# Sixteen tokens move from the dense expert sum to row fetches, and one-hots are built four tokens at a time

## The chip, the cores and the metric

The kernel runs on one core of a Trainium2 chip. The core has a matmul engine (TensorE, PE in the rows; its weight loads are PEld), a vector engine (VectorE, DVE), an activation engine (ScalarE, ACT), GpSimd (POOL) and SyncE (SP); 16 DMA engines move data for all of them. The metric is the device time of one execution in microseconds (us), as the median of several runs.

## The reference, cut to what matters

Two transformer blocks run one after the other on 512 tokens of 1024 numbers. The change lies in the feed-forward part of the first block: 16,384 experts, each one row of `u_tab` and one row of `v_tab`. For each token and each of 8 heads the 16 best experts are found through product keys (an expert's number is `128*i1 + i2`); `g` are their softmaxed scores, the gates. All is float32.

```python
        eidx = jnp.take_along_axis(cidx, fpos, axis=-1).reshape(C, PEER_HEADS * PEER_TOPK)
        g = jax.nn.softmax(fv, axis=-1).reshape(C, PEER_HEADS * PEER_TOPK)
        u = u_tab[eidx]
        a = jax.nn.gelu(jnp.einsum('ted,td->te', u, hb).astype(jnp.float32), approximate=False)
        coef = (g * a).astype(hb.dtype)
        vv = v_tab[eidx]
        return jnp.einsum('te,ted->td', coef, vv)
```

So each token uses 128 expert rows of each table. A convolution block and an attention block follow, which need the whole result.

## The kernel before, in words

`phase_peer` computes these experts in two ways. The first `ND` = 384 tokens are **dense**: every expert is computed for all of them, and a gate matrix that is mostly zeros picks what counts. The last 128 tokens are **fetched**: one token sits on each partition, and for each of its 128 experts an indirect DMA issued by GpSimd brings one row per token (128 rows of 4 KB, 512 KB in all) into a buffer.

The dense tokens pass through two stages of 128 units each. In the **first stage** a unit is 128 experts of `u`: a slab of 512 KB is loaded (`_load`), split into a high and a low half (`_split`: `whi` on ScalarE, `wlo` on VectorE), multiplied with the tokens (`gemm_w`: 8 blocks of rows, three matmuls each by `mm3`, with `ND` columns moving), and its Gelu goes to `ga`, which is written to DRAM (`Ad`). In the **second stage** a unit is 128 experts of `v`: `weight(i)` multiplies gates (`gg`, read back from DRAM, or the last two chunks `near`, which stay in SBUF) with `ga` and splits the product (`w_hi`, `w_lo`); then 8 blocks of `mm3` add into the 8 PSUM banks `y`, again with `ND` columns moving. The last two units run as one, bank by bank. Then each bank gets the fetched tokens' sum by a transpose of `yG` into its last columns (L1280), and VectorE adds the bank to the residual `xres2` (L1281), from which the convolution starts (`act`, L384 and L385).

The gate matrix is made during the first stage, in steps of four tokens in `gates(tb)`: per token one-hots of `i1` (times the gate) and of `i2`, and a matmul of the two (`flush`, L1099), in chunks of 32 tokens (`gc`, to DRAM as `Gd`).

The fetches are one generator, `gather()`: for each head 16 fetches of `u` rows into `ug`, each multiplied with the token `hG` and summed by one VectorE instruction (L1143), a Gelu over the 16 sums, then 16 fetches of `v` rows into `vg`, each added into `yG` by one VectorE instruction (L1153). `ug` and `vg` are rings of 3 buffers each; a fetch waits on GpSimd until the VectorE instruction that used its buffer is over. `c.pump2` hands out steps of it, unit by unit, in both stages; `c.in_turn` allows such a VectorE instruction no earlier than the split of its unit; `c.drain2()` hands out the rest before the last unit. The final order of the instructions on each engine is set by a scheduler when the kernel is built; on the chip each of these engines takes its instructions in that order.

## Time and profile before

| | |
|---|---|
| median of 3 runs | 2439.63 us (2437.38 to 2447.22) |
| the profiled execution, its own time | 2439.81 us, span 2438.0 us |
| TensorE clock granted over the span | 0.992 of full speed |
| first stage of the experts | about 427 to 1025 us |
| second stage of the experts | about 1026 to 1569 us |

An engine's busy time is the sum over its instructions with overlaps counted once. A row with an arrow tells what an engine waited for. In a timeline, a row with "x4" is four instructions merged.

### The profile page before, as it was taken

To read this page: it belongs to the slowest core of one execution; us is meant where nothing else is said; L and a number is where in the kernel's file an instruction comes from. 1 tells how busy PE (TensorE), PEld (TensorE's weight loads), DVE (VectorE), ACT (ScalarE), POOL (GpSimd) and SP (SyncE) were. 2 spreads that over 40 slices of the span, in tenths; PEclk is the share of its full clock that TensorE was granted. 3 is DMA by queue.
4 is the path that set the end of the run, shared out by engine and by line. 5 is a ranking of instruction groups with operands and counts; after the bars stand their busy time and mean duration, and the time that the engine had idled before them with its cause. 6 is when DMAs were issued, how large, how long until landed. Compare 5 with 4: busy or idle time off the path is not lost.

```text
span 2438.0 us, 37744 instructions
## 1 busy us (share of the span) xinstructions
PE 2399.8 (98%) x13677; PEld 2175.6 (89%) x13677; DVE 1861.4 (76%) x4195; ACT 1153.5 (47%) x2372; POOL 361.4 (15%) x334
## 2 busy tenths in 40 slices
PE   7999999999999999999999999999999999999998
PEld 4886888999999999999999999988888888887777
DVE  7897589999998878878888887865555447586774
ACT  3468433434777858733333333432222233445762
POOL 0000000024334333224332221100000000000000
PEclk8999999999999999999999999999999999999999
DMA  7460152569899998899999998333222234221002
GB/s 276 144 217 10 61 191 88 172 232 330 325 315 319 368 347 309 293 392 350 363 346 348 338 343 306 118 105 102 96 95 95 97 112 172 69 71 51 2 1 78
DMA packets 170938, 490.47 MB, mean 201 GB/s; under 512 B 15473, under 2 KB 62513, under 8 KB 169089
## 3 DMA queue, kind: packets, MB, share of 16 engines
q1 hardware_dynamic: 123744, 295.48, 35.0%
q0 software_dynamic: 44992, 189.68, 21.5%
q10 hardware_dynamic: 2016, 2.91, 0.4%
q8 instruction: 108, 1.77, 0.3%
q14 instruction: 78, 0.63, 0.1%
HBM read 437.15 MB, written 50.86 MB: 200 GB/s over the span
## 4 chain that ended last, share of the span: by engine, by line
PE 93%; DMA 3%; DVE 2%; ACT 2%; issue 0%; SPq 0%; DVEq 0%; ACTq 0%
PE mm L178 8%; PE mm L180 8%; PE mm L179 8%; PE s L180 8%; PE s L179 8%; PE s L178 8%; PE pt L178 4%; PE pt L180 4%; PE pt L179 4%; PE gp L1099 3%; PE z L178 2%; PE z L179 2%; PE z L180 2%; PE o L1724 2%; PE o L180 2%; PE o L178 2%
## 5 line engine op out<-in xcount | busy, mean ns | idle before, releaser
L102 ACT ACTIVATE whi<-wraw 128x1024 fp32r<-128x1024 f32 (+2 forms) x292 | 305.2, 1046 | 548.4 <-PE mm L179 171.3
L103 DVE TENSOR_TENSOR wlo<-wraw,whi 128x1024 fp32r<-128x1024 f32 (+2 forms) x292 | 350.5, 1202 | 95.2 <-ACT whi L102 93.4
L179 PE MATMUL mm<-act,whi 128*128 128x384 f32 (+2 forms) x1176 | 402.5, 343 | 0.0
L180 PE MATMUL mm<-act,wlo 128*128 128x384 f32 (+2 forms) x1176 | 401.6, 343 | 0.1
L178 PE MATMUL mm<-act,whi 128*128 128x384 f32 (+2 forms) x1176 | 399.2, 343 | 0.7 <-DVE xres L862 0.7
L102 ACT ACTIVATE whi<-act 128x1024 fp32r<-128x1024 f32 x126 | 133.5, 1061 | 327.6 <-issue 314.0
L180 PEld LDWEIGHTS mm<-act,wlo 128*128 128x128 f32 x1176 | 221.6, 188 | 4.4 <-DVE wlo L103 0.5
L179 PEld LDWEIGHTS mm<-act,whi 128*128 128x128 f32 x1176 | 221.6, 188 | 3.9
L178 PEld LDWEIGHTS mm<-act,whi 128*128 128x128 f32 x1176 | 220.0, 188 | 4.8 <-issue 0.8
L103 DVE TENSOR_TENSOR wlo<-act,whi 128x1024 fp32r<-128x1024 f32 x126 | 154.1, 1224 | 82.6 <-ACT whi L102 81.3
L1135 POOL DMA_INDIRECT ug<-in_peer_u_rows_dram,eiG x128 | 159.1, 1243 | 368.7 <-DVE ug L1143 252.2
L1135 POOL DMA_INDIRECT vg<-in_peer_v_rows_dram,eiG x128 | 159.4, 1246 | 294.7 <-DVE yG L1153 192.1
L179 PE MATMUL s<-w_lo,whi 128*128 128x384 f32 x512 | 171.3, 335 | 0.2 <-DVE w_lo L224 0.2
L178 PE MATMUL s<-w_hi,whi 128*128 128x384 f32 x512 | 170.6, 335 | 0.6 <-ACT ga L1209 0.6
L180 PE MATMUL s<-w_hi,wlo 128*128 128x384 f32 x512 | 170.6, 335 | 0.0
L1153 DVE SCALAR_TENSOR_TENSOR yG<-vg,gG,yG 128x1024 f32<-128x1024 f32 x127 | 162.3, 1278 | 8.9 <-DMA vg<-in_peer_v_rows_dram,eiG 8.7
L1143 DVE SCALAR_TENSOR_TENSOR ug<-ug,hG 128x1024 f32<-128x1024 f32 x128 | 155.5, 1217 | 11.8 <-DMA ug<-in_peer_u_rows_dram,eiG 11.7
L178 PE MATMUL s<-act,whi 128*128 128x512 f32 x344 | 134.5, 392 | 0.0
L180 PE MATMUL s<-act,wlo 128*128 128x512 f32 x344 | 134.1, 390 | 0.2 <-DVE wlo L103 0.2
L179 PE MATMUL s<-act,whi 128*128 128x512 f32 x344 | 133.7, 390 | 0.0
L1113 DVE TENSOR_SCALAR oh<-iof,idxT 128x128 f32<-128x128 f32 x384 | 116.9, 350 | 6.9 <-PE gp L1099 6.7
L1099 PE MATMUL gp<-oh,oh 128*128 128x128 f32 x768 | 115.1, 275 | 0.0
(684 smaller groups left out, 5735.2 us busy)
## 6 DMA issues: line engine op xcount, KB each, us to landing
wraw<-in_peer_u_dram SPq DMA_DIRECT2D x128, 512.0 KB, 5.1
act<-in_peer_v_rows_dram SPq DMA_DIRECT2D x126, 512.0 KB, 6.9
wraw<-in_a_in_dram SPq DMA_DIRECT2D x64, 512.0 KB, 3.2
Ad<-ga POOLq DMA_DIRECT2D x30, 768.0 KB, 7.8
ga<-Ad SPq DMA_DIRECT2D x30, 768.0 KB, 9.8
Gd<-gc POOLq DMA_DIRECT2D x10, 2048.0 KB, 10.2
gg<-Gd SPq DMA_DIRECT2D x32, 640.0 KB, 8.0
wraw<-in_ada_w_dram SPq DMA_DIRECT2D x32, 512.0 KB, 4.6
```

The source lines that it names most:

```text
L102: self.first = first = self.nc.scalar.activation(hi[:, :n], r[:, :n], AF.Copy)
L103: self.last = self.nc.vector.tensor_tensor(lo[:, :n], r[:, :n], hi[:, :n].bitcast(F32), op=OP.subtract)
L178: mm(out, lh, rh, start=start, stop=False)
L179: mm(out, lh, rl, start=False, stop=False)
L180: self.product = mm(out, ll, rh, start=False, stop=stop)
L1099: nc.tensor.matmul(gp[:, j, :], o1, o2, start=True, stop=True)
L1113: nc.vector.tensor_scalar(o1, iof, idxT[:, 0, t:t + 1], idxT[:, 2, t:t + 1], op0=OP.is_equal, op1=OP.mult)
L1135: nc.gpsimd.indirect_dma_start(out=t, out_offset=None, in_=tab, in_offset=bass.IndirectOffsetOnAxis(ap=eiG[:, j:j + 1], axis=0))
L1143: c.in_turn(nc.vector.scalar_tensor_tensor(u, u, 1.0, hG, op0=OP.mult, op1=OP.mult, accum_out=aG[:, j:j + 1]))
L1153: op = nc.vector.scalar_tensor_tensor(yG, v, gG[:, j:j + 1], yG, op0=OP.mult, op1=OP.add)
L1724: nc.tensor.matmul(o[64 * h:64 * h + 64, t], V[:, b, v], pair[h][br][:, b * P:(b + 1) * P], start=False, stop=br == 1 and b == qb, skip_gr ...
```

## The change

`ND` becomes 368. Tokens 368 to 383 (`XT` = 16) are fetched too. They use all 128 partitions as 8 groups (`RX`) of 16: a group holds the 16 tokens once more with another 16 of their 128 experts. So their numbers and gates are spread by 2 x 8 small DMAs on GpSimd's queue (`eiX`, `gX`), `hX` holds each token 8 times, and 16 fetches of `u` and 16 of `v` (`gather_x`) serve them, after those of `gather()`. At the end a matmul with `fold`, 16 columns wide, sums the 8 groups into the bank. All fetches, of `u` and `v` and of both generators, now share one ring `fetched` of `NFE` = 4 buffers. The one-hots of `i1` are built for four tokens by one VectorE instruction, without the gate; the gate enters the one-hot of `i2`: on ScalarE as scale and bias of the Relu for three of four tokens, on VectorE for the fourth. The core of the diff:

```diff
-ND = 384
+ND = 368
+N3 = S - P
+XT = N3 - ND
+RX = P // XT
...
+NFE = 4
...
+            if (tb + 1) * P > ND:
+                eix = pool.tile([P, P], I32, name="eix", bufs=1)
+                nc.vector.tensor_copy(eix, ev)
+                for r in range(RX):
+                    to, sl = slice(r * XT, (r + 1) * XT), slice(r * P // RX, (r + 1) * P // RX)
+                    nc.gpsimd.dma_start(eiX[to, :], eix[P - XT:P, sl])
+                    nc.gpsimd.dma_start(gX[to, :], gv[P - XT:P, sl])
+                c.later2(gather_x())
...
+                    o1s = rpool.tile([P, 4, P], F32, name="oh1", bufs=2)
+                    nc.vector.tensor_tensor(o1s, iof[:, None, :].to_broadcast([P, 4, P]),
+                                            idxT[:, 0, t0:t0 + 4, None].to_broadcast([P, 4, P]), op=OP.is_equal)
                     for j in range(4):
...
-                        nc.vector.tensor_scalar(o1, iof, idxT[:, 0, t:t + 1], idxT[:, 2, t:t + 1], op0=OP.is_equal,
-                                                op1=OP.mult)
...
-                            nc.scalar.activation(o2, d_, AF.Relu, bias=1.0, scale=-1.0)
+                            nc.scalar.activation(o2, d_, AF.Relu, bias=idxT[:, 2, t:t + 1], scale=idxT[:, 3, t:t + 1])
...
+        def rows(tab, idx, j):
+            t = gpool.tile([P, D], F32, name="fetched", bufs=NFE)
...
+        def gather_x():
+
+            n = P // RX
+            for j in range(n):
+                u = rows(a["peer_u_rows"], eiX, j)
+                c.in_turn(nc.vector.scalar_tensor_tensor(u, u, 1.0, hX, op0=OP.mult, op1=OP.mult,
+                                                         accum_out=aX[:, j:j + 1]))
+                yield 1.2
+            nc.scalar.activation(aX, aX, AF.Gelu)
+            nc.vector.tensor_tensor(gX, gX, aX, op=OP.mult)
+            for j in range(n):
+                v = rows(a["peer_v_rows"], eiX, j)
+                if j == 0:
+                    op = nc.vector.tensor_scalar(yX, v, gX[:, 0:1], None, op0=OP.mult)
+                else:
+                    op = nc.vector.scalar_tensor_tensor(yX, v, gX[:, j:j + 1], yX, op0=OP.mult, op1=OP.add)
+                c.in_turn(op)
+                yield 1.2
...
+        c.later(rows_of_x())
...
                 if i == P - 1:
-                    nc.tensor.transpose(y[m][:, ND:S], yG[:, m * P:(m + 1) * P], c.ident)
+                    nc.tensor.matmul(y[m][:, ND:N3], yX[:, m * P:(m + 1) * P], fold, start=True, stop=True)
+                    nc.tensor.transpose(y[m][:, N3:S], yG[:, m * P:(m + 1) * P], c.ident)
```

The change also moves instructions. On VectorE, at the end of the second stage, this stood before (`wlo<-act` is the split of a slab of `v`, `wlo<-wraw` that of the convolution's first slab, `yG<-vg` a fetched row's sum):

```order
L103 TENSOR_TENSOR wlo<-act,whi 128x1024
L1153 SCALAR_TENSOR_TENSOR yG<-vg,gG,yG 128x1024
L224 TENSOR_TENSOR w_lo<-w,w_hi 128x384
L1153 SCALAR_TENSOR_TENSOR yG<-vg,gG,yG 128x1024
L103 TENSOR_TENSOR wlo<-act,whi 128x1024
L224 TENSOR_TENSOR w_lo<-w,w_hi 128x384
L1153 SCALAR_TENSOR_TENSOR yG<-vg,gG,yG 128x1024
L103 TENSOR_TENSOR wlo<-wraw,whi 128x1024
L1281 SCALAR_TENSOR_TENSOR xres<-s,mod,xres 128x512 x4
L1281 SCALAR_TENSOR_TENSOR xres<-pt,mod,xres 128x512
L385 SCALAR_TENSOR_TENSOR act<-xres,gains,act 128x512 x2
```

and this stands there now (`fetched,aX<-` are the row products of `gather_x`, `yX<-` its sums):

```order
L1174 TENSOR_TENSOR gG<-gG,aG 128x16
L1180 SCALAR_TENSOR_TENSOR yG<-fetched,gG,yG 128x1024 x2
L107 TENSOR_TENSOR wlo<-act,whi 128x1024
L228 TENSOR_TENSOR w_lo<-w,w_hi 128x368
L1180 SCALAR_TENSOR_TENSOR yG<-fetched,gG,yG 128x1024 x2
L107 TENSOR_TENSOR wlo<-wraw,whi 128x1024
L1180 SCALAR_TENSOR_TENSOR yG<-fetched,gG,yG 128x1024 x12
L1225 SCALAR_TENSOR_TENSOR fetched,aX<-fetched,hX 128x1024 x16
L1229 TENSOR_TENSOR gX<-gX,aX 128x16
L1233 TENSOR_SCALAR yX<-fetched,gX 128x1024
L1235 SCALAR_TENSOR_TENSOR yX<-fetched,gX,yX 128x1024 x15
L1344 SCALAR_TENSOR_TENSOR xres<-s,mod,xres 128x512 x4
```

Before, one sum of fetched rows (L1153) stands behind the last split of a slab of `v` and none behind the convolution's first split; now 2 + 12 + 16 + 16 = 46 instructions on fetched rows stand behind the former and 44 of them behind the latter. In the second stage itself, between the first and the last split of a `v` slab, 124 such instructions stood before and 111 do now.

On TensorE, before, the transposes of `yG` stood among the matmuls of the last two units; the end of these units, up to the convolution's first matmul (128x512):

```order
L1280 MATMUL o<-ident,yG 128x128
L178 MATMUL z<-w_hi,whi 128x384
L179 MATMUL z<-w_lo,whi 128x384
L180 MATMUL z<-w_hi,wlo 128x384
L178 MATMUL z<-w_hi,whi 128x384
L179 MATMUL z<-w_lo,whi 128x384
L180 MATMUL z<-w_hi,wlo 128x384
L1280 MATMUL z<-ident,yG 128x128
L178 MATMUL s<-act,whi 128x512
```

and now (`z<-` is the eighth bank's, `s<-fold,yX` the first bank's sum over groups):

```order
L182 MATMUL z<-w_hi,whi 128x368
L183 MATMUL z<-w_lo,whi 128x368
L184 MATMUL z<-w_hi,wlo 128x368
L1342 MATMUL s<-fold,yX 128x16
L1343 MATMUL s<-ident,yG 128x128
L1342 MATMUL s<-fold,yX 128x16
L1343 MATMUL s<-ident,yG 128x128
```

All matmuls of the second stage now stand ahead of the eight pairs of fold and transpose, and the convolution's behind them.

On GpSimd's queue 130 fetches stood behind the last write of `Ad` before, most of them `u` and `v` in turns; now there are 168, in runs of 16 `u` and 16 `v`, those of `gather_x` last, with nothing between them.

## Rows read from the trace of the kernel before

**Rows 1.** The page, part 1: busy time, share and count of each engine.
```profile
PE 2399.8 (98%) x13677; PEld 2175.6 (89%) x13677; DVE 1861.4 (76%) x4195; ACT 1153.5 (47%) x2372; POOL 361.4 (15%) x334
```

**Rows 2.** Three stretches: from:to, length, busy (count) by engine, PEclk, DMA share, GB/s.
```profile
488.00:549.00 61.00, 61.00 (x354) 61.00 (x353) 60.93 (x145) 21.57 (x30) 14.26 (x12) 1.00 0.66 231
1220.00:1281.00 61.00, 61.00 (x354) 61.00 (x353) 53.56 (x99) 20.85 (x30) 20.79 (x18) 1.00 0.95 347
1647.00:1708.00 61.00, 61.00 (x271) 50.54 (x270) 33.03 (x41) 15.90 (x18) 0.00 (x0) 1.00 0.30 95
```

**Rows 3.** Timeline of TensorE, 320 columns: start us, us, engine, line, operation.
```profile
115.30 0.31 PE L180 MATMUL ps<-whi,act_lo 128*128 128x320 f32 x1
...
118.68 0.31 PE L179 MATMUL ps<-wlo,act_hi 128*128 128x320 f32 x1
```

**Rows 4.** Groups by line and form (count, busy us, mean ns, idle before).
```profile
L178 PE MATMUL mm<-act,whi 128*128 128x384 f32 x1024 | 347.9, 340 | 0.0
...
L1113 DVE TENSOR_SCALAR oh<-iof,idxT 128x128 f32<-128x128 f32 x384 | 116.9, 350 | 6.9 <-PE gp L1099 6.7
...
L1099 PE MATMUL gp<-oh,oh 128*128 128x128 f32 x768 | 115.1, 275 | 0.0
```

**Rows 5.** The chain that ended last, one gate step (start us, us, work, count).
```profile
613.40 0.89 PE gp L1099 x8
```

**Rows 6.** Timeline of VectorE, end of the second stage.
```profile
1550.28 1.28 DVE L1153 SCALAR_TENSOR_TENSOR yG<-vg,gG,yG 128x1024 f32<-128x1024 f32 x1
...
1556.54 1.22 DVE L103 TENSOR_TENSOR wlo<-act,whi 128x1024 fp32r<-128x1024 f32 x1
...
1558.15 1.28 DVE L1153 SCALAR_TENSOR_TENSOR yG<-vg,gG,yG 128x1024 f32<-128x1024 f32 x1
...
1560.71 1.22 DVE L103 TENSOR_TENSOR wlo<-wraw,whi 128x1024 fp32r<-128x1024 f32 x1 [1.28 <-ACT whi L102]
1563.83 2.73 DVE L1281 SCALAR_TENSOR_TENSOR xres<-s,mod,xres 128x512 f32<-128x512 f32 x4 [1.90 <-PE s L1280]
```

**Rows 7.** Timeline of TensorE, end of the second stage.
```profile
1560.05 0.51 PE L178 MATMUL s<-w_hi,whi 128*128 128x384 f32 x2
...
1568.70 0.27 PE L1280 MATMUL z<-ident,yG 128*128 128x128 f32 x1
```

**Rows 8.** Timeline of GpSimd (POOL), the last fetch of the second stage.
```profile
1551.83 0.98 POOL L1135 DMA_INDIRECT vg<-in_peer_v_rows_dram,eiG  x1 [0.66 <-DVE yG L1153]
```

**Rows 9.** Tile vg, 1530 to 1560 us: issue to landing.
```profile
DMA to landing us min/median/max: 4.1/5.0/5.4
```

**Rows 10.** Tile vg, 1165 to 1230 us: issue to landing.
```profile
DMA to landing us min/median/max: 6.5/8.1/9.5
```

**Rows 11.** Timeline of GpSimd, two bursts of fetches.
```profile
493.65 1.00 POOL L1135 DMA_INDIRECT ug<-in_peer_u_rows_dram,eiG  x1 [10.54 <-DVE fp L1009]
...
501.43 1.95 POOL L1135 DMA_INDIRECT vg<-in_peer_v_rows_dram,eiG  x1 [0.30 <-issue]
503.37 0.59 POOL L1211 DMA_DIRECT2D Ad<-ga  x1
...
1130.25 1.96 POOL L1135 DMA_INDIRECT vg<-in_peer_v_rows_dram,eiG  x1 [0.30 <-issue]
...
1137.07 1.92 POOL L1135 DMA_INDIRECT ug<-in_peer_u_rows_dram,eiG  x1 [0.30 <-DVE w L1251]
```

**Rows 12.** Timeline of GpSimd, a fetch issued at 1489 us.
```profile
1489.07 1.86 POOL L1135 DMA_INDIRECT vg<-in_peer_v_rows_dram,eiG  x1 [11.62 <-DVE yG L1153]
```

**Rows 13.** Timeline of VectorE, the same place.
```profile
1487.52 2.60 DVE L1153 SCALAR_TENSOR_TENSOR yG<-vg,gG,yG 128x1024 f32<-128x1024 f32 x2
```

**Rows 14.** Timeline of ScalarE, the Gelu over 16 columns.
```profile
1485.69 0.20 ACT L1146 ACTIVATE aG<-aG 128x16 f32<-128x16 f32 x1
```

**Rows 15.** Timeline of TensorE after an idle stretch.
```profile
101.23 0.52 PE L179 MATMUL ps<-wlo,act_hi 128*128 128x384 f32 x1
...
103.80 0.52 PE L178 MATMUL ps<-whi,act_hi 128*128 128x384 f32 x1
```

More of the change, by code (lines that the diff above doesn't have):

```diff
@@ L1086, in select @@
                 nc.tensor.transpose(pt[:, i * P:(i + 1) * P], src, c.ident)
[L1087 removed]
+            tt = slice(tb * P, min(ND, (tb + 1) * P))
+            n = tt.stop - tt.start
+            pv = pt.rearrange("p (i t) -> p i t", i=4)[:, :, 0:n]
+            nc.scalar.activation(idxT[:, 0:3, tt], pv[:, 0:3], AF.Copy)
+            nc.scalar.activation(idxT[:, 3, tt], pv[:, 2], AF.Copy, scale=-1.0)
+            nc.scalar.activation(neg_i2[:, tt.start // 4:tt.stop // 4],
+                                 pv[:, 1].rearrange("p (q j) -> p q j", j=4)[:, :, 3], AF.Copy, scale=-1.0)
             sel_left.discard(tb)
@@ L1101, in flush @@
                 nc.scalar.activation(dst, gp.rearrange("p t i -> p i t"), AF.Copy)
-            for ch in range(4):
+            for ch in range(-(-(min(ND, (tb + 1) * P) - tb * P) // 32)):
                 gc = gcpool.tile([P, P, 32], F32, name="gc", bufs=2)
@@ L1141, in gather @@
                 for j in range(16 * h, 16 * h + 16):
-                    u = rows(a["peer_u_rows"], j, "ug", 3)
+                    u = rows(a["peer_u_rows"], eiG, j)
                     c.in_turn(nc.vector.scalar_tensor_tensor(u, u, 1.0, hG, op0=OP.mult, op1=OP.mult,
@@ L1148, in gather @@
                 for j in range(16 * h, 16 * h + 16):
-                    v = rows(a["peer_v_rows"], j, "vg", 3)
+                    v = rows(a["peer_v_rows"], eiG, j)
                     if j == 0:
@@ L1178, in rows_of_h, with rows_of_x @@
                 nc.scalar.activation(hG[:, hf * S:(hf + 1) * S], pt, AF.Copy)
-        sel_left = set(range(ND // P))
+        def rows_of_x():
+            for hf in range(2):
+                pt = psp.tile([P, S], F32, name="tp", bufs=1)
+                for k in range(4):
+                    kk = 4 * hf + k
+                    hs = pool.tile([P, RX, XT], F32, name="stmp", bufs=2)
+                    hh, hl = [act[i][:, kk, None, ND:N3].bitcast(F32).to_broadcast([P, RX, XT]) for i in range(2)]
+                    nc.vector.tensor_tensor(hs, hh, hl, op=OP.add)
+                    yield 0.2
+                    nc.tensor.transpose(pt[:, k * P:(k + 1) * P], hs.rearrange("p r t -> p (r t)"), c.ident)
+                nc.scalar.activation(hX[:, hf * S:(hf + 1) * S], pt, AF.Copy)
+        def gather_x():
[15 more added lines that the diff above has]
+                yield 1.2
+        sel_left = set(range(N3 // P))
         pend = None
@@ L1249, in weight @@
             for n in range(NF_, NC_):
-                t = slice(n * 32, n * 32 + 32)
-                nc.vector.tensor_tensor(w[:, t], near[n][:, order[g] * 4 + j, :], ga[:, j, t], op=OP.mult)
+                t = slice(n * 32, min(ND, n * 32 + 32))
+                nc.vector.tensor_tensor(w[:, t], near[n][:, order[g] * 4 + j, 0:t.stop - t.start], ga[:, j, t], op=OP.mult)
             hi = vpool.tile([P, ND], F32R, name="w_hi", bufs=3)
```

39 lines of the change are left out of this document (23 added, 16 removed).

## The prediction

> **What bounds the kernel now.** I read the busy times of the page first, then three stretches side by side, then the end of the second expert stage instruction by instruction. TensorE is busy 98% of the span [rows 1], which by itself says little, so I look at how closely its matmuls follow one another. In a stretch of the first stage and in one of the second it starts 354 matmuls in 61 us and is never idle [rows 2]: 172.3 ns each with 384 columns. In the convolution it starts 271 in 61 us, 225.1 ns each with 512 columns. A matmul of 320 columns follows the next after 147.0 ns (23 of them from 115.30 to 118.68 us) [rows 3]. So the time is 147, 172 and 225 ns for 320, 384 and 512 columns: about 0.40 to 0.41 ns per column on top of some 15 ns, all at the granted clock of 1.00, that is 2.4 GHz. TensorE sets the time of both stages, by its columns. VectorE is nearly full too in the first stretch (60.93 of 61 us) but not in the second (53.56), and TensorE waits for it in neither [rows 2]. The question is what happens where the stages end: there TensorE needs the fetched sum, which VectorE makes.
>
> **The change part by part: TensorE's gain.** Sixteen columns fewer are worth 16 x 0.40 = 6.4 ns between 320 and 384, and 6.6 between 384 and 512; I take 6.5. Each stage has 128 units x 8 blocks x 3 matmuls = 3072 (the first stage is the group of 1024 in [rows 4] and two like it), so 6144 x 6.5 ns = 39.9 us. The gate step issues 768 matmuls for 384 tokens [rows 4], 2 per token, 8 in 0.89 us [rows 5], 0.111 us each: 16 tokens fewer save 32 x 0.111 = 3.6 us. `rows_of_x` adds 8 transposes of the same form, 16 issues, 1.8 us. Net gain: 41.7 us.
>
> **What costs nothing.** The new one-hot of 512 columns is not in the trace. It lies between one old one-hot of 128 columns, 0.35 us [rows 4], and a two-operand instruction of 1024 columns, 1.22 us [rows 6]; near half of the latter, 0.6 us. 92 of those, 55 us, replace 368 x 0.35 = 129 us, in the stage in which VectorE is full. TensorE doesn't wait for VectorE there, so this is worth nothing now, and covers the small instructions that the change adds there. ScalarE's Relu keeps its count, and its busy time is 22 us of 61 [rows 2]. Sixteen small DMAs enter GpSimd's queue in two runs of 8, at about 0.59 us each as for a write of `Ad` [rows 11], 4.7 us a run, and delay the fetch behind them. The 256 row sums lie between 493.65 [rows 11] and 1558.15 us [rows 6], one in 4.2 us, so that four landed buffers hold some 17 us of them, and I count nothing; if that cover is gone, VectorE's split is late and TensorE waits for a few us, at most the two runs, 9 us.
>
> **What is added at the end.** This is the large term. Before, VectorE had one row sum left after its last split (the one at 1558.15 us), split the convolution's first slab until 1560.71 + 1.22 = 1561.93 us, and began the first bank's addition 1.90 us later, at 1563.83, when TensorE had that bank [rows 6]. TensorE was then still at the last two units, which run from about 1560.0 to 1568.7 us [rows 7], and went on without a gap. In the order of the change 44 row sums stand between that split and that addition. VectorE takes them in that order: in the trace its last instructions come as the order of before has them. Nor can they start earlier, because the splits ahead of them wait for TensorE to free the halves (this one for ScalarE, as its row says). The convolution needs the additions, so TensorE's own 8 us run out and it waits.
>
> How long is one of the 44? Call it r. A buffer of the ring passes through: release by VectorE to issue by GpSimd, 0.27 us (1550.28 + 1.28 = 1551.56 us [rows 6], issued at 1551.83 [rows 8]); issue to landing, L; the row sum, 1.28 us. Four buffers give r = (0.27 + L + 1.28) / 4. At the end of the stage L was 4.1 at the least and 5.0 in the median [rows 9], in the middle of the stage, with the DMA engines 95% busy [rows 2], 8.1 in the median [rows 10]. So r is 1.41, 1.64 or 2.41 us. VectorE alone needs 2.60 - 1.28 = 1.32 us for a sum behind a sum [rows 13]; the row products of `u` don't wait for one another and may come a little closer, so I take 1.25 as its least. GpSimd issued fetches back to back at (501.43 - 493.65) / 5 = 1.56 us and, in a stretch in which VectorE was full, at (1137.07 - 1130.25) / 3 = 2.27 us [rows 11]. At the end the stage's own loads are over, but the four fetches share the DMA engines: I take L = 5.0, nearest to the end's own row, and r = 1.65, and keep 1.25 and 2.41 as bounds.
>
> The sum: 44 rows are ten rounds of the ring and a last four at VectorE's own pace of about 1.2 us, 40 r + 4.8 = 70.8 us. Between the `u` and `v` rows of `gather_x` stand a Gelu of 0.20 us [rows 14], a small product and the hand-overs to and from ScalarE, at 0.27 us as above: 1.0 us. Fold and transpose of the first bank: 4 issues x 0.111 = 0.4 us. Less the 1.9 us that VectorE waited there before. TensorE comes back from a long idle stretch, and after a mixed stretch early in the run it took 9 matmuls of 384 columns at half the clock, 1.2 GHz (8 x 0.321 us from 101.23 to 103.80 [rows 15]), about 0.15 us each too long: 1.5 us with the one beside them. Together 70.8 + 1.0 + 0.4 - 1.9 + 1.5 = 71.8 us. In terms of r this is 40 r + 5.8 us. The other additions of VectorE and the convolution's start then follow as before, only later.
>
> Net: 71.8 - 41.7 = 30.1 us slower. The profiled execution took 2439.81 us (0.2 us off the median of the runs shown), so 2470 us. What r decides: at 1.25 us the sum gives 2454, at 1.41 us 2460, at 2.27 us 2495, at 2.41 us 2500.
>
> **A rule against the change.** Beside the ring stands GpSimd itself. A fetch issued at 1489.07 us took 1.86 us to issue [rows 12], where 0.98 is usual [rows 8]; VectorE was in the second of two row sums until 1490.1 us [rows 13], and the issue ended 0.8 us after that. The Trainium skill, "SBUF — State Buffer", section "SBUF: two separate sides", says that a VectorE instruction with two inputs in SBUF and a GpSimd instruction that reads SBUF exclude each other: whichever starts first holds the shared ports for its whole length. By that rule every issue that starts within a row sum waits for its end, and this row agrees. It gives a result of its own, the first rival.
>
> **The rivals.**
> *GpSimd paces the tail.* If each release at 0.27 us finds the next row sum already running, each issue lasts about 1.2 us longer, and issues come as in the stretch with VectorE full, 2.27 us apart [rows 11]. Then 40 x 2.27 + 5.8 = 96.6, and 2495 us. For it: the release comes just then. Against it: at 1.65 us VectorE is idle a quarter of the time, from 1.2 to 1.65 us after a row sum's start, and a release at 1.28 + 0.27 = 1.55 us falls into that gap.
> *VectorE paces the tail.* If the fetches land as fast as VectorE sums (L of 3.45 us or less), r is 1.25, the tail costs 40 x 1.25 + 5.8 = 55.8 us, and 14 us remain: 2454 us, at the edge of what can be told from no change. Against it: no fetch of the last 30 us landed in less than 4.1 us [rows 9].
> *The small DMAs also cost.* The cover of four buffers fails and both runs show, 9 us: 2479 us. For it: a run waits for VectorE first. Against it: the count above.
> *VectorE reaches the tail early: not slower.* If VectorE got through its last splits long before TensorE needs them, the row sums would run beside the second stage and only the gain be left: 2398 us. The lead decides: with 30 us more of it than counted the loss is gone. Against it: in the trace the last split ends at 1557.8 us [rows 6] and TensorE at 1568.7 [rows 7], a lead of 11 us, held there by buffers that the change leaves alone.
>
> **How the numbers follow.** Forecast, r between 1.35 and 2.0: 0.62, at 2470. GpSimd paces: 0.17. Small DMAs on top: 0.05. VectorE paces: 0.12, of which I put 0.08 within what a measurement of this kernel can tell from no change, about 0.5% or 12 us. VectorE early: 0.04. Slower by more than that: 0.62 + 0.17 + 0.05 + 0.04 = 0.88; within: 0.08; faster: 0.04. The range leaves out the last case and takes in both bounds of r, 2454 and 2500, with a few us for the gain's own uncertainty below: from 2450 to 2500 us.
>
> **What would show it.** In the profile of the change: 166 ns from matmul to matmul in both stages, without idle time; the last matmul of the second stage about 42 us earlier than before; then TensorE idle for some 65 us, ended by VectorE's sum `yX`; 44 row sums in that time at about 1.65 us, with VectorE waiting for fetches; a TensorE clock at half speed just after. I am wrong if the row sums come at another pace, if VectorE reaches them earlier than the end of the stage, or if TensorE waits within the stages, where I count nothing.

## The result, and the profile of the changed kernel

The changed kernel takes 2504.4 us (median of 4 runs, 2503.1 to 2510.3) against 2439.4 us, 1.027 times as long (95% interval 1.025 to 1.028). The forecast was 2470 us, its range 2450 to 2500. The profiled execution has a span of 2502.1 us, 64.1 us more than before. Part 1 of the page answers to [rows 1]; of part 2 the slices of TensorE and of its clock are shown, 62.6 us a digit.

```profile
PE 2371.0 (95%) x13669; PEld 2142.7 (86%) x13669; DVE 1868.6 (75%) x3958; ACT 1186.5 (47%) x2353; POOL 418.8 (17%) x382
...
PE   7999999999999999999999997099999999999998
...
PEclk8999999999999999999999998599999999999999
```

TensorE falls from 98% to 95%: it is idle 131.1 us instead of 38.2. Most of the 92.9 us more lie in one place, the slice with a 0, where its clock goes down too. Three stretches of the same view as [rows 2] (the last is the convolution, 64 us later than there):

```profile
488.00:549.00 61.00, 61.00 (x368) 61.00 (x367) 60.93 (x166) 24.37 (x33) 8.51 (x8) 1.00 0.64 222
1220.00:1281.00 61.00, 61.00 (x366) 61.00 (x365) 50.87 (x95) 22.01 (x31) 14.78 (x13) 1.00 0.96 338
1711.00:1772.00 61.00, 61.00 (x271) 50.51 (x270) 33.22 (x42) 16.22 (x18) 0.00 (x0) 1.00 0.29 95
```

In these stretches all is as forecast: 368 and 366 matmuls in 61 us, 165.8 and 166.7 ns each, no idle time. The view of waits of TensorE (us in total, times, longest), its largest wait and two more that the kernel before does not have:

```profile
PE s L1342 <- DVE yX L1235: 79.6, 1, 79.6
...
PE s L182 <- ACT whi L106: 5.5, 1, 5.5
...
PE sc L1188 <- ACT s__3451 L1191: 3.8, 1, 3.8
```

The timeline of TensorE gives the borders: the first matmul of 368 columns, the first of the second stage, the last of it, the first bank's `fold`, and the convolution. Under it the first two of the kernel before; for its end see [rows 7].

```profile
421.32 0.33 PE L182 MATMUL mm<-act,whi 128*128 128x368 f32 x1
...
1023.68 0.44 PE L182 MATMUL s<-w_hi,whi 128*128 128x368 f32 x1 [0.57 <-ACT ga L1269]
...
1546.52 0.33 PE L184 MATMUL z<-w_hi,wlo 128*128 128x368 f32 x1
1626.45 0.61 PE L1342 MATMUL s<-fold,yX 128*128 128x16 f32 x2 [79.60 <-DVE yX L1235]
...
1630.73 0.77 PE L182 MATMUL s<-act,whi 128*128 128x512 f32 x1
```

```profile
411.61 0.42 PE L178 MATMUL mm<-act,whi 128*128 128x384 f32 x1
...
1034.50 0.44 PE L178 MATMUL s<-w_hi,whi 128*128 128x384 f32 x1 [0.58 <-ACT ga L1209]
```

The first stage begins 9.7 us later than before, lasts 602.4 us instead of 622.9, and the second ends at 1546.85 instead of 1568.86 us. So only 22.0 us are gained there, not 41.7. (The table ahead of the prediction has 427 and 1026 us for the begin of the two stages before; the timeline has 411.6 and 1034.5. And 1.6 of the 9.7 us are there already when the first transpose of `rows_of_h` begins, at 325.67 us instead of 324.04.) Then TensorE waits 79.6 us for the last sum of `yX`. VectorE in that time, answering to [rows 6]:

```profile
1540.17 1.22 DVE L107 TENSOR_TENSOR wlo<-wraw,whi 128x1024 fp32r<-128x1024 f32 x1
1541.31 2.72 DVE L1180 SCALAR_TENSOR_TENSOR yG<-fetched,gG,yG 128x1024 f32<-128x1024 f32 x2
...
1623.79 2.61 DVE L1235 SCALAR_TENSOR_TENSOR yX<-fetched,gX,yX 128x1024 f32<-128x1024 f32 x2 [0.46 <-DMA fetched<-in_peer_v_rows_dram,eiX]
1627.39 2.73 DVE L1344 SCALAR_TENSOR_TENSOR xres<-s,mod,xres 128x512 f32<-128x512 f32 x4 [0.99 <-PE s L1343]
```

The convolution's split ends at 1541.39 us, 20.5 us earlier than before; behind it stand 44 row sums, to 1626.40 us; the first addition begins 86.0 us after the split, where it was 1.9. Together 84.1 - 20.5 + 0.5 = 64.1 us; the 0.5 is what is left over, and TensorE's slow start behind the wait would be such a cost.

### The profile page after: what moved, and what is told of

Its sections match the earlier page's. It is cut to its first block, busy times and chain, and to the rows that moved or that the text cites. A ratio compares the mean times of both kernels' runs of the same rounds, so it can differ in the third digit from the quotient of the medians.

```text
span 2502.1 us, 37446 instructions
## 1 busy us (share of the span) xinstructions
PE 2371.0 (95%) x13669; PEld 2142.7 (86%) x13669; DVE 1868.6 (75%) x3958; ACT 1186.5 (47%) x2353; POOL 418.8 (17%) x382
## 4 chain that ended last, share of the span: by engine, by line
PE 84%; DVE 7%; DMA 4%; issue 2%; ACT 2%; POOL 1%; SPq 0%; DVEq 0%; POOLq 0%; ACTq 0%
PE s L184 7%; PE s L183 7%; PE s L182 7%; PE mm L184 7%; PE mm L182 7%; PE mm L183 6%; PE pt L183 4%; PE pt L184 4%; PE pt L182 4%; PE gp L1123 3%; PE o L1787 2%; PE z L183 2%; PE z L184 2%; PE z L182 2%; PE ps L183 2%
## 5 line engine op out<-in xcount | busy, mean ns | idle before, releaser
L184 PE MATMUL mm<-act,wlo 128*128 128x368 f32 (+2 forms) x1176 | 397.9, 339 | 0.8 <-DVE wlo L107 0.8
L182 PE MATMUL mm<-act,whi 128*128 128x368 f32 (+2 forms) x1176 | 395.9, 340 | 2.0 <-ACT qT L1252 0.7
L183 PE MATMUL mm<-act,whi 128*128 128x368 f32 (+2 forms) x1176 | 396.6, 338 | 0.0
L1160 POOL DMA_INDIRECT fetched<-in_peer_u_rows_dram,eiG x128 | 162.2, 1267 | 337.8 <-DVE fetched L1170 192.1
L107 DVE TENSOR_TENSOR wlo<-act,whi 128x1024 fp32r<-128x1024 f32 x126 | 154.3, 1224 | 84.5 <-ACT whi L106 79.6
L1160 POOL DMA_INDIRECT fetched<-in_peer_v_rows_dram,eiG x128 | 165.4, 1292 | 277.1 <-DVE yG L1180 153.6
L1180 DVE SCALAR_TENSOR_TENSOR yG<-fetched,gG,yG 128x1024 f32<-128x1024 f32 x127 | 162.6, 1280 | 15.6 <-DMA fetched<-in_peer_v_rows_dram,eiG 14.8
L182 PE MATMUL s<-w_hi,whi 128*128 128x368 f32 x512 | 168.2, 329 | 6.1 <-ACT whi L106 5.5
L183 PE MATMUL s<-w_lo,whi 128*128 128x368 f32 x512 | 169.9, 332 | 0.0
L184 PE MATMUL s<-w_hi,wlo 128*128 128x368 f32 x512 | 169.4, 331 | 0.0
L1170 DVE SCALAR_TENSOR_TENSOR fetched<-fetched,hG 128x1024 f32<-128x1024 f32 x128 | 155.5, 1218 | 7.9 <-DMA fetched<-in_peer_u_rows_dram,eiG 7.8
L1144 ACT ACTIVATE oh<-ohd,idxT 128x128 f32<-128x128 f32 x276 | 128.4, 488 | 9.3 <-PE gp L1123 8.0
```

The lines of the kernel that those rows point to most:

```text
L107: self.last = self.nc.vector.tensor_tensor(lo[:, :n], r[:, :n], hi[:, :n].bitcast(F32), op=OP.subtract)
L182: mm(out, lh, rh, start=start, stop=False)
L183: mm(out, lh, rl, start=False, stop=False)
L184: self.product = mm(out, ll, rh, start=False, stop=stop)
L1144: nc.scalar.activation(o2, d_, AF.Relu, bias=idxT[:, 2, t:t + 1], scale=idxT[:, 3, t:t + 1])
L1160: nc.gpsimd.indirect_dma_start(out=t, out_offset=None, in_=tab, in_offset=bass.IndirectOffsetOnAxis(ap=idx[:, j:j + 1], axis=0))
```

## The experiments

Times are medians, beside the kernel before on the same chip (2440 to 2441 us in each group). "Idle at the end" is TensorE's wait for the fetched sums behind the second stage.

| run | us | ratio, 95% interval | idle at the end |
|---|---|---|---|
| changed kernel | 2504.4 | 1.025 to 1.028 | 79.6 |
| e1_earlier | 2485.1 | 1.015 to 1.020 | none |
| e2_ring5 | 2482.6 | 1.015 to 1.019 | 63.1 |
| e3_no_x_rows | 2441.9 | 0.999 to 1.001 | 14.2 |
| e4_onehots_only | 2447.1 | 1.002 to 1.004 | none |
| e5_half_sums | 2465.0 | 1.009 to 1.012 | none |
| e6_x_rows_late | 2490.9 | 1.019 to 1.023 | 58.8 |
| e7_load_order | 2499.3 | 1.022 to 1.026 | 82.0 |
| e8_one_operand | 2501.6 | one run | 77.7 |
| e9_before_products | 2474.4 | 1.012 to 1.016 | none |
| e10_six | 2461.3 | 1.008 to 1.010 | 23.1 |
| e11_six_forced | 2472.1 | 1.012 to 1.015 | none |
| e12_products_ahead | 2476.6 | 1.013 to 1.017 | none |
| e13_together | 2466.2 | 1.009 to 1.013 | none |
| e14_splits_behind | 2434.2 | 0.997 to 0.999 | none |
| e15_earlier_start | 2429.5 | 0.995 to 0.998 | none |
| e16_lag12 | 2422.2 | 0.991 to 0.994 | none |

**What the 32 fetches and the ring cost.**

```diff
-                c.later2(gather_x())
+                nc.vector.tensor_copy(yX, hX)
```


> The changed kernel without the 32 fetches and sums of the 16 further tokens (their experts' output is left out; yX is filled with a copy of hX). 12 of 256 row sums stand behind the convolution's first split instead of 44. If the 32 fetches are what costs: TensorE's idle time at the end of the second stage falls by 32 x 1.93 = 62 us from 79.6 to about 18 us and the time to 2442 us, which is no faster than the kernel before, because 12 sums still stand there and the 16 us lost at the two other places stay lost. If the fetches also hold up the loads of the stages, TensorE gains there too and it comes below 2435 us.

2441.9 us, and 14.2 us idle: the 32 rows cost 62 us. With 12 sums still behind the split the rest of the change is worth nothing. In this run the trace lists how long a fetch takes from issue to landing (12 sums, ring of four):

```profile
DMA to landing us min/median/max: 5.0/5.5/6.9
```

```diff
-NFE = 4
+NFE = 5
-        yX = gpool.tile([P, D], F32, name="yX")
+        yX = hX
```


> The changed kernel with a ring of five buffers in place of four (yX takes hX's place, which pays for the fifth); 41 row sums instead of 44 stand behind the convolution's first split. Ring theory, a buffer's round trip sets the pace: in the tail of the changed kernel it is about 0.65 (release to issue) + 5.5 (issue to landing) + 1.28 (the sum) = 7.4 us, so 1.5 us a sum with five buffers: 36 x 1.5 + 5 x 1.25 + 1 = 61 us of row sums instead of 85, 2480 us. GpSimd theory, its issues set the pace (0.94 us, and 1.8 to 1.95 us where one begins inside a row sum): the pace stays at 1.9 us and only the 3 sums fewer show, 2498 us. Transfer theory, four fetches at once already fill the DMA engines (share 0.80): a fifth only makes each landing longer, at most 1/0.8 faster, 2488 us or more.

2482.6 us is the ring's figure, but in part by luck: the pace is 1.69 us, not 1.5 (41 sums, the first begun at 1536.86, the last at 1604.39), and the second stage became 6 us shorter, which the forecast does not have. The landings became longer:

```profile
DMA to landing us min/median/max: 5.4/6.0/6.4
```

The DMA share is 0.89 from 1545 to 1600 us, and 0.81 with four buffers. So the round trip sets the pace, and it became longer with more fetches under way: by 0.5 us to the landing, and by as much from release to issue (1.1 us in the mean, 0.65 counted). An issue takes 1.26 us in the mean and the next begins 0.30 us later at the soonest; that is 1.56 of every 1.69 us, so with five buffers GpSimd's queue is nearly full too. The wait at the start of the second stage fell from 5.5 to 1.6 us.

```diff
-                    op = nc.vector.scalar_tensor_tensor(yX, v, gX[:, j:j + 1], yX, op0=OP.mult, op1=OP.add)
+                    op = nc.vector.tensor_scalar(yX, v, gX[:, j:j + 1], None, op0=OP.mult)
```


> The changed kernel with the last 15 row sums of yX as a product of one tensor by a column (the accumulation is left out, so 15 of the 16 slots are missing from yX). Same order. If a fetch that begins inside a row sum is held until that sum ends because the sum reads two tensors, the 16 issues that lie beside these products all take about 0.94 us (in the changed kernel their median is 1.12 and the longest 1.86 us). If GpSimd is held by any VectorE instruction, or by the DMA side, long ones stay. By the ring the pace of these 15 is (0.3 + 5.5 + 0.75) / 4 = 1.6 us instead of 1.93, and the time 2499 us.

Of the 13 issues from 1595.13 us on 9 take 0.93 or 0.94 us; the longest take 1.28 and 1.19, so a one-operand product holds GpSimd too: two operands are not what it takes. GpSimd's timeline, then VectorE's:

```profile
1595.13 1.19 POOL L1160 DMA_INDIRECT fetched<-in_peer_v_rows_dram,eiX  x1 [0.30 <-issue]
...
1600.61 1.28 POOL L1160 DMA_INDIRECT fetched<-in_peer_v_rows_dram,eiX  x1 [3.05 <-DVE yX L1235]
```

```profile
1594.75 0.75 DVE L1233 TENSOR_SCALAR yX<-fetched,gX 128x1024 f32<-128x1024 f32 x1 [0.27 <-DMA fetched<-in_peer_v_rows_dram,eiX]
1597.34 0.75 DVE L1235 TENSOR_SCALAR yX<-fetched,gX 128x1024 f32<-128x1024 f32 x1 [1.83 <-DMA fetched<-in_peer_v_rows_dram,eiX]
...
1601.02 0.75 DVE L1235 TENSOR_SCALAR yX<-fetched,gX 128x1024 f32<-128x1024 f32 x1 [1.00 <-DMA fetched<-in_peer_v_rows_dram,eiX]
...
1605.42 0.75 DVE L1235 TENSOR_SCALAR yX<-fetched,gX 128x1024 f32<-128x1024 f32 x1 [2.44 <-DMA fetched<-in_peer_v_rows_dram,eiX]
...
1622.52 0.75 DVE L1235 TENSOR_SCALAR yX<-fetched,gX 128x1024 f32<-128x1024 f32 x1 [0.51 <-DMA fetched<-in_peer_v_rows_dram,eiX]
```

The pace of the 15 is (1622.52 - 1597.34) / 14 = 1.80 us, not 1.6, though the issues of 1.8 us and more are gone. But it holds one wait that is neither the ring nor a long issue: by the order of the ring the fetch at 1600.61 us could take the buffer of the product begun at 1597.34, which was over at 1598.09; what held it for 2.5 us more isn't shown. From its own product on (1605.42 us) ten come 1.71 us apart, in the changed kernel the same ten 1.85 ((1625.11 - 1606.57) / 10). By the ring the shorter products alone are worth (1.28 - 0.75) / 4 = 0.13 of these 0.14 us. So GpSimd's long issues do not set the pace, and little is seen of them here.

**One-hots alone**, in the kernel before (with the gates on ScalarE, as in the change):

```diff
-                        nc.vector.tensor_scalar(o1, iof, idxT[:, 0, t:t + 1], idxT[:, 2, t:t + 1], op0=OP.is_equal,
-                                                op1=OP.mult)
+                    nc.vector.tensor_tensor(o1s, iof[:, None, :].to_broadcast([P, 4, P]),
+                                            idxT[:, 0, t0:t0 + 4, None].to_broadcast([P, 4, P]), op=OP.is_equal)
```

> The kernel before (384 dense tokens, two rings of three) with nothing but the new one-hots: four tokens at a time on VectorE, the gates on ScalarE. The prediction's claim, VectorE's saving of some 70 us in the first stage is worth nothing because TensorE never waits for VectorE there: 2439 us, within 5 us. Rival, VectorE is what holds the stages through the order of the splits: faster by 10 us or more, 2429 us or less.

2447.1 us: slower by 0.3%, outside both forecasts. TensorE loses nothing in the first stage, with or without the relief, but waits 3.7 us at the start of the second for a split whose load landed late; SP's queue has the reload of `Ad` ahead of these loads, as in the changed kernel (e7, below). Relief for VectorE was worth nothing, and the order that came with it cost a little.

**The two small losses.**

```diff
         c.later(rows_of_h())
-        c.later(rows_of_x())
...
             c.later(select(tb))
+            if tb == 0:
+                c.later(rows_of_x())
```


> The changed kernel with one line moved: rows_of_x is written behind the second token block's selection instead of ahead of the first scores. 34 row sums instead of 44 stand behind the convolution's first split. If rows_of_x is what made TensorE wait at 361 to 370 us (3.8 us for the scores' eviction, then half the clock), that loss of about 8 us goes: 2504 - 10 x 1.93 - 8 = 2477 us, TensorE idle about 60 us at the end of the second stage. If that wait has another cause it stays: 2485 us.

The selection lost nothing now: TensorE is busy 125.98 us from 300 to 427 us, as before the change (120.95 in the changed kernel). From the first transpose of `rows_of_h` to the first stage it takes 87.4 us, 87.6 before the change and 95.7 in the changed kernel. `rows_of_x` was the cause, at 8 us. Idle at the end falls to 58.8 us. But the gates now reach to the end of the first stage, which lasts 23 us longer than in the changed kernel: TensorE waits there for ScalarE's one-hots and runs at half the clock in part (0.99 granted over the stage). Of the 27 us of gain forecast 14 are lost again.

```profile
PE gp L1123 <- ACT oh L1144: 9.9, 18, 2.2
```

```diff
-                nc.sync.dma_start(ga.rearrange("p j t -> p (j t)"), Ad[grp])
+                c.in_turn(nc.sync.dma_start(ga.rearrange("p j t -> p (j t)"), Ad[grp]), c.load)
```


> The changed kernel with one line changed: the reload of a group of Ad stands behind the load of weights written last, so that on SP's queue the first 7 loads of the second stage go out ahead of it. 46 row sums instead of 44 stand behind the convolution's first split, 4 us more. If the late first load is what cost TensorE 5.5 us and half the clock behind it at 1031 to 1043 us, some 8 us go: 2500 us, and the 5.5 us wait falls to 2 us or less. If it is not the order of these loads, the wait stays: 2508 us.

2499.3 us, and the wait is 2.2 us instead of 5.5, close to the forecast. The rows of the changed kernel (SP's queue, then ScalarE) and, last, of the kernel before:

```profile
1021.65 2.63 SPq L1295 DMA_DIRECT2D ga<-Ad  x1
1024.33 0.42 SPq L97 DMA_DIRECT2D wraw<-in_a_in_dram  x1
1024.85 20.94 SPq L97 DMA_DIRECT2D act<-in_peer_v_rows_dram  x12
```

```profile
1036.41 1.06 ACT L106 ACTIVATE whi<-act 128x1024 fp32r<-128x1024 f32 x1 [3.82 <-DMA act<-in_peer_v_rows_dram]
```

```profile
1033.93 5.13 SPq L93 DMA_DIRECT2D act<-in_peer_v_rows_dram  x7
1040.51 0.33 SPq L1235 DMA_DIRECT2D ga<-Ad  x1
```

In the changed kernel the reload of `Ad` holds SP's queue for 2.63 us and the first loads of the second stage go out 1.7 us after the first stage's last matmul (1023.12 us), to land 11.6 us later; before, the reload stood behind 7 of them.

**Moving the sums into the stages.**

```diff
     def in_turn(self, op, prev=None):
+        if prev is None:
+            self.sums.append(op)
...
+        if key[0] in "UV" and len(self.sums) > 8:
+            self.in_turn(self.last, self.sums[-9])
...
-GU, BU, GUL, BUL, GV = 1.6, 2.4, 1.6, 2.4, 1.6
+GU, BU, GUL, BUL, GV = 2.0, 2.4, 2.0, 2.4, 1.4
```


> The changed kernel with the row sums put earlier: each split of an expert slab on VectorE stands behind the row sum that was written 8 before it, and the rates at which row sums are written are 2.0 in the first stage and 1.4 in the second. In the order 143 of the 288 sums then stand before the second stage, 145 in it, none behind it (126, 116 and 46 in the changed kernel). Theory A, the tail is only a matter of order and the stages have room: TensorE's idle 79.6 us at the end of the second stage go to about 2 us and nothing comes back, 2504 - 78 = 2426 us. Theory B, the DMA engines have no room (share 0.95 to 0.97 over most of the second stage): 29 more fetches at the tail's 1.5 us of engine time each are 43 us in that stage, TensorE waits there for the loads of its weights for about that long, 2504 - 78 + 43 = 2469 us. Row sums within 0.1 us of their 1.22 and 1.28 us in both.

2485.1 us: the tail was gone and came back inside the stages. The first lasts 44 us longer than in the changed kernel; TensorE is idle 30.6 us in it, in waits of several kinds, the longest (8.4 us) for a load of weights. In the second it is idle 24.4 us, in waits for VectorE's splits (22.9 us, 18 times), not for loads. Neither theory fits. Then half-length sums on the same order (`H2 = D // 2`, each sum on `[:, 0:H2]`):

> The kernel of e1_earlier with every row sum on half of its 1024 columns (the other half of the fetched rows' output is left out); the fetches are as large as before. In the order 144 sums stand before the second stage, 144 in it, none behind. In e1_earlier the tail was gone and TensorE lost as much inside the two stages. Theory VectorE: the sums, 1.22 and 1.28 us each, stand on VectorE in front of the splits for which TensorE waits; at about 0.65 us each these waits nearly vanish, and of some 75 us lost in the stages at most 20 stay: 2430 us or less. Theory transfers: the fetches hold up the loads of the weights; these are unchanged, TensorE still waits, 2470 us or more.

2465.0 us, between the two. The stretch, TensorE's wait, and VectorE's own wait from 1024 to 1560 us:

```profile
1100.00:1500.00 400.00, 382.31 (x2235) 377.16 (x2235) 286.68 (x636) 145.33 (x191) 168.65 (x109) 0.99 0.93 348
PE s L191 <- DVE wlo L109: 18.7, 18, 1.9
...
DVE w_lo L235 <- ACT w_hi L234: 128.3, 99, 3.6
```

VectorE is busy only 287 of 400 us, and TensorE still waits for it: VectorE stands at the head of its queue, 128 us in all, at a `w_lo` whose other half ScalarE can't write before TensorE frees a buffer, and the split that TensorE needs is queued behind it. So in this stage it is neither VectorE's load nor loads of weights; what the rows point to is the order in an in-order queue. The kernels e9 and e12 to e14 test that.

```diff
-            nc.vector.tensor_tensor(w[:, :F_].rearrange("p (c t) -> p c t", c=NF_), gg[:, :, j, :],
+            wop = nc.vector.tensor_tensor(w[:, :F_].rearrange("p (c t) -> p c t", c=NF_), gg[:, :, j, :],
...
+            if len(c.sums) > 8:
+                c.in_turn(wop, c.sums[-9])
```


> The changed kernel with the row sums of the second stage put earlier in another way than in e1_earlier: not the split of a weight slab, but the product of gates and activations for the next unit stands behind the row sum written 8 before it. In the order 126 sums stand before the second stage, 161 in it, 1 behind. In e1_earlier TensorE waited for VectorE's splits, 18 times in the second stage, and still did with half-length sums. Theory order: that came from the splits, which that edit itself put behind other work in VectorE's queue; with the splits left free TensorE's waits in the second stage stay under 10 us, and the time is about 2504 - 78 + 10 = 2436 us. Theory transfers: 45 more fetches in that stage, at some 1.5 us each of the DMA engines' time, do not fit into its 40 us of free engine time; TensorE waits there for 25 us or more, for loads or for splits behind late fetches: 2455 us or more.

2474.4 us: now the products are late (31.7 us, 22 times), and the splits are not, but for the first one of the stage (6.6 us). VectorE waited for fetched rows 2 us in this stage.

```diff
-            if i + 1 < P:
-                weight(i + 1)
+            if i + 3 < P:
+                weight(i + 3)
```


> e9_before_products with one thing more: the products of the second stage are made three units ahead of TensorE instead of one (five buffers for their halves instead of three). 126 sums before the second stage, 159 in it, 3 behind. In e9_before_products TensorE waited 40 us in that stage for halves of the products. Theory lead: VectorE and the DMA engines have the room, only the lead of one unit is too short where a sum stands ahead; with three units these waits fall under 10 us and the time from 2474 to about 2440 us. Theory transfers: fetches and loads together exceed what the DMA engines move there, so a longer lead is used up once and TensorE waits as long as before, for loads or splits: 2465 us or more.

2476.6 us: the lead alone changes nothing. With ring, `rows_of_x` and the reload mended as well:

> e12_products_ahead with a ring of five (yX in hX's place), rows_of_x written behind all four selections, and the reload of Ad behind the loads of weights. 131 sums before the second stage, 154 in it, 3 behind; the gates' products end before the second stage, as in the changed kernel. If all holds: the kernel before less the gain of 41.7 us, and some 8 us of small waits, 2439 - 42 + 8 = 2405 us, faster than the kernel before. If the second stage's transfers are full, 25 us or more stay in it: 2425 us or more.

2466.2 us. TensorE loses nothing more up to 1100 us (3 us), and 31 of 400 us in the second stage:

```profile
1100.00:1500.00 400.00, 369.31 (x2137) 361.68 (x2136) 331.15 (x606) 133.62 (x178) 120.28 (x114) 0.99 0.94 342
PE s L186 <- ACT w_hi L231: 37.4, 22, 4.4
```

```diff
+        if key[0] == "V" and len(self.sums) > 8:
+            self.in_turn(self.last, self.sums[-9])
...
-            if len(c.sums) > 8:
-                c.in_turn(wop, c.sums[-9])
...
-            if i + 3 < P:
-                weight(i + 3)
+            if i + 4 < P:
+                weight(i + 4)
```


> e13_together with the products four units ahead and seven buffers for their halves, and the split (not the product) of the second stage behind the row sum written 8 before it. 131 sums before the second stage, 152 in it, 5 behind. In the second stage VectorE's time is full in the kernel before and in the changed one alike: busy 339 and 335 of 400 us, and nearly all the rest at the head of its queue, waiting for ScalarE's half of a split. If that waiting is what a sum could use, an order that makes products early and splits late lets TensorE go on: waits under 10 us in the stage, 2415 us. If the engines of the transfers are what is full, the order is of no use: 2455 us or more, with the DMA share at 0.95 or more and waits behind fetches or loads.

2434.2 us, 32 us less than e13 with nearly as many sums in the stage:

```profile
1100.00:1500.00 400.00, 379.29 (x2208) 373.50 (x2207) 351.05 (x655) 144.56 (x187) 194.95 (x122) 0.99 0.97 361
PE s L190 <- DVE wlo L108: 22.2, 20, 2.6
```

The DMA share is 0.97 at 361 GB/s (0.94 and 342 in e13). So the transfers had room for these sums, and what was bad was the order, or the short lead of the products that went with it. 22.2 us of waits for splits are left. From here on only the rates and the lag:

```diff
-GU, BU, GUL, BUL, GV = 1.6, 2.4, 1.6, 2.4, 1.6
+GU, BU, GUL, BUL, GV = 1.6, 2.8, 1.6, 3.0, 1.6
...
-                c.gemm_w(("peer_q", hp), o, act, pump=4.0)
+                c.gemm_w(("peer_q", hp), o, act, pump=5.0)
...
-        if key[0] == "V" and len(self.sums) > 8:
-            self.in_turn(self.last, self.sums[-9])
+        if key[0] == "V" and len(self.sums) > 12:
+            self.in_turn(self.last, self.sums[-13])
```

> e14_splits_behind with the selection written sooner (5.0 for 4.0 in the queries, 2.8 and 3.0 for 2.4 in the first stage), so that fetching begins sooner: 141 sums before the second stage instead of 131, 147 in it instead of 152, none behind it. In e14 TensorE still waited 22 us for splits in the second stage and lost nothing in the first. If that is a matter of how many sums the stage has to take, 5 of 152 fewer take a few us off, at most the 10 us that 5 x 1.9 are in the tail: 2425 to 2432 us. If the first stage then loses what the second gains (as in e1_earlier, some 23 us for 17 sums): 2440 us or more.

> e15_earlier_start with the split behind the row sum written 12 before it instead of 8. In the order 2 sums more stand behind the second stage. If late row sums are what the splits wait behind, a longer lag lets them go earlier: TensorE's waits for splits in the second stage fall by a third or more, against 4 us more behind it: 2420 to 2428 us. If VectorE's time is simply full, the lag changes nothing: as e15, or 4 us more.

2429.5 and 2422.2 us; the second is 0.7% faster than the kernel before. The waits for splits fell from 18.5 to 15.5 us, by a sixth and not by a third; the clock, which fell twice in the second stage of e15 (to 0.99 over it), stayed at 1.00 in e16. What it still loses:

```profile
1100.00:1500.00 400.00, 384.52 (x2261) 379.45 (x2260) 352.86 (x665) 147.06 (x193) 190.63 (x121) 1.00 0.98 365
PE s L190 <- DVE wlo L108: 15.5, 15, 2.3
```

**Two that missed.** Ring of six, `rows_of_x` as in e6, the reload as in e7, and the selection's rates (the diff is e10's; e11 keeps 2.4 and has the products as in e9; both have 5.0 for 4.0 in the queries):

```diff
-GU, BU, GUL, BUL, GV = 1.6, 2.4, 1.6, 2.4, 1.6
+GU, BU, GUL, BUL, GV = 1.6, 2.6, 1.6, 2.4, 1.6
...
-NFE = 4
+NFE = 6
```

> What the experiments so far point to, together: a ring of six (yX in hX's place, two smaller pools), rows_of_x behind the second block's selection, the reload of Ad behind the loads of weights, and the selection written a little earlier (5.0 for 4.0, 2.6 for 2.4), so that fetching begins earlier. 143 sums stand before the second stage, 125 in it, 20 behind it, 18 of them behind the convolution's first split. By the ring the tail is 12 x 1.4 + 6 x 1.25 + 1 = 25 us; with some 4 us of other waits kept: 2439 - 41.7 + 25 - 1.9 + 3 + 4 = 2427 us, 0.5% faster than the kernel before. If earlier fetching holds up the stages as in e1_earlier, 17 more sums in the first stage cost about 1 us each again: 2445 us.

> As e10_six, but with the selection's rate 2.4, and the product of the next unit in the second stage behind the row sum written 14 before it: 141 sums before the second stage, 144 in it, 3 behind. If the second stage takes 20 more sums than in e10_six for nothing, the tail's 25 us go too: 2405 us. If its transfers are full, TensorE waits there for about as long as the tail was: 2427 us.

2461.3 and 2472.1 us. The tail of e10 was 23.1 us, close to the 25 forecast. But the gates stand at the end of the first stage, which lasts 31 and 38 us longer than in the changed kernel: from 900 to 1100 us TensorE is idle 14 and 15 us (waits for one-hots and for products behind them) and its clock falls to 0.90 and 0.88. The selection's rates are not the cause: e6 loses 23 us there at the old rates, and e15 and e16 lose nothing at higher ones (600.2 and 601.9 us, 602.4 in the changed kernel). What e6, e10 and e11 share is `rows_of_x` behind the second selection; e13 to e16 have it behind all four.

## Why the prediction was wrong, point by point

The forecast's sum was -41.7 + 71.8 = 30.1 us; it came to 64.1.

- **TensorE's columns: right.** 6.5 ns a matmul were counted; the stretches give 6.5 and 5.6 ns. The first stage became 20.5 us shorter, where the forecast has 20.0 and the gates' 3.6.
- **"Net gain: 41.7 us": the first step that failed.** The gain was taken whole from matmul times, with "I count nothing" for waits outside the two stretches read. 22.0 us reached the end of the second stage; of the 19.7 missing, 7.9 are lost ahead of the first stage, 3.0 in it and 8.8 in the second. `rows_of_x` was counted with its 8 transposes, 1.8 us, but in the selection, where VectorE is full, it made TensorE wait 3.8 us and then run six matmuls 0.43 us apart at a granted clock of 0.50, 1.2 GHz: the first stage starts 9.7 us late, 8.1 of them from here (the other 1.6 are older). The second stage starts with a load 11.6 us under way instead of 8.5: 5.5 us of waiting, then some 16 matmuls 0.31 instead of 0.17 us apart. e6 and e7 show both causes. The stretch of the slow matmuls:

```profile
364.00:370.00 6.00, 4.90 (x15) 4.03 (x16) 6.00 (x43) 1.56 (x3) 0.00 (x0) 0.50 0.24 84
```

- **One-hots and small DMAs at nothing: nearly.** The new one-hot takes 0.69 us (0.6 counted). The two runs of DMAs took 7.8 and 7.2 us, not 4.7 (from 704.6 and from 742.8 us). From 427 to 1024 us TensorE is idle 2.0 us in all, with the sixteen DMAs in that time; that rival falls. By e4 the one-hots cost 6 us, all of it in the second stage (540.3 us instead of 534.4), where the load is late.
- **44 sums behind the split: right, and so was the mechanism.** e3 prices them: 62 us for 32.
- **r = 1.65: the second step that failed, a term too small.** 44 sums took 85.1 us, 1.93 us each; in the prediction's own terms, 40 r + 4.8 + 1.0, r is 1.98. That lies inside the 1.35 to 2.0 that it gave, and by its sum would make 2483 us: what carried the time out of the range is the gain. The round trip was put at 0.27 + 5.0 + 1.28. Measured on the changed kernel, from issue to the start of the sum 5.7 us in the median (31 sums that waited for their landing; e3 lists 5.5 to the landing), from release to issue 0.76 in the mean, and 1.26 for a sum: 7.7 / 4 = 1.93. L = 5.0 was read while the ring was not full of fetches (DMA share 0.41 from 1530 to 1560 us, 0.81 in the tail); four at once lengthen it, five lengthen it more (e2). In all the first addition came 84.1 us later instead of 70.3: 13.8 us. With the gain missing at the split, 41.7 - 20.5 = 21.2, less the 1.0 us by which the remainder of 0.5 is under the 1.5 counted for the clock, these are the 34.0 us.
- **The rival "GpSimd paces": in part.** Its issues do meet the sums. GpSimd and VectorE in the tail:

```profile
1571.56 0.94 POOL L1160 DMA_INDIRECT fetched<-in_peer_u_rows_dram,eiX  x1 [1.19 <-DVE fetched L1225]
1573.23 1.80 POOL L1160 DMA_INDIRECT fetched<-in_peer_u_rows_dram,eiX  x1 [0.73 <-DVE fetched L1225]
1575.34 1.45 POOL L1160 DMA_INDIRECT fetched<-in_peer_u_rows_dram,eiX  x1 [0.30 <-issue]
1577.10 1.47 POOL L1160 DMA_INDIRECT fetched<-in_peer_u_rows_dram,eiX  x1 [0.30 <-issue]
```

```profile
1571.73 1.23 DVE L1225 SCALAR_TENSOR_TENSOR fetched<-fetched,hX 128x1024 f32<-128x1024 f32 x1 [0.44 <-DMA fetched<-in_peer_u_rows_dram,eiX]
...
1573.00 1.23 DVE L1225 SCALAR_TENSOR_TENSOR fetched<-fetched,hX 128x1024 f32<-128x1024 f32 x1
...
1574.76 1.23 DVE L1225 SCALAR_TENSOR_TENSOR fetched<-fetched,hX 128x1024 f32<-128x1024 f32 x1 [0.53 <-DMA fetched<-in_peer_u_rows_dram,eiX]
...
1576.53 1.23 DVE L1225 SCALAR_TENSOR_TENSOR fetched<-fetched,hX 128x1024 f32<-128x1024 f32 x1 [0.54 <-DMA fetched<-in_peer_u_rows_dram,eiX]
```

  The issue at 1573.23 us begins in a sum and ends 0.80 us after that sum; the next two queue behind it, 1.1 us after their release instead of 0.27. The Trainium skill, "SBUF — State Buffer", section "SBUF: two separate sides", has this rule, and in this direction the trace agrees. In the other it does not: the sum at 1571.73 us began inside the issue of 1571.56, took its usual 1.23 us and lengthened nothing. Held issues are worth the 0.49 us of the release, 0.12 us a sum. But the pace was 1.93 us, not 2.27, and in e8, with most long issues gone, hardly better than the shorter products make it. The longer landing, 0.7 us or 0.18 a sum, was the larger part; how much of it is again the long issues, behind which it is longer (5.9 us in the median for issues of 1.4 us and more, 5.5 for the others), isn't told apart.
- **"VectorE early" didn't happen.** The last split of `v` was over 9.6 us ahead of TensorE's last matmul (1537.29 and 1546.85 us), before 11, and behind it the sums waited for fetches. Whether its 2398 us can be had isn't shown; with the sums in the stages e16 reaches 2422.

What stays open: e14 differs from e13 in three things (which instruction stands behind the sums, the products' lead, their buffers), and which of them did it wasn't told apart; whether the 15.5 us of waits left in e16 come from VectorE's queue or from transfers (share 0.98); and what held the one fetch in e8 (the same fetch is late in the changed kernel, at 1600.68 us, 2.0 us after the sum that used its buffer).

## What to carry to other kernels

A change that shortens the bound stages also shortens the cover for work that runs beside them: ask of each such row of work where it goes, and price it at its pace without cover, with as many transfers under way as there will be. An idle engine with an in-order queue is not room: see at what it waits, and what stands behind. In the changed kernel VectorE, from 1100 to 1500 us (its row, then its waits):

```profile
1100.00:1500.00 400.00, 400.00 (x2389) 400.00 (x2388) 334.67 (x630) 146.19 (x202) 98.28 (x90) 1.00 0.96 339
DVE wlo L107 <- ACT whi L106: 59.7, 72, 1.6
DVE wlo L107 <- issue: 3.6, 6, 0.6
```

Of 400 us it is busy 335 and 63 at the head of its queue, at a split; sums put there helped only once products went ahead and splits behind, with more buffers (e14). And a gain read from a stretch in the middle is checked at the borders of its stages.

## What the runs showed of the hardware

A fetch that GpSimd issues inside a two-operand sum ends 0.80 us after it, up to 1.95 us in all; a sum that begins inside an issue doesn't lengthen it (the issue at 1571.56 us, a sum from 1571.73: 0.94 us). One-operand products (e8) held it in both cases: the issue at 1595.13 us began inside a product that ended at 1595.50 and ended 0.82 us after it; in the one at 1600.61 us a product began at 1601.02, and it ended 0.12 us after that product's end (so did those at 1612.08 and 1613.51). Products that began 0.7 us into an issue or later lengthened nothing (the issues at 1596.62 and 1604.67 us). After 5.5 us of idle time TensorE came back at half the clock, for 5 us, and in e7 after 2.2 us, for 3.4 us; in e16 a wait of 2.3 us (at 1449 us) left the clock at 1.00.
